# Moving the seventh of seven Strassen products between the fourth and the fifth, with its weight sum written over another tile

## The chip, the cores and the metric

The kernel runs on one core of a Trainium2 chip. The metric is device time in microseconds (us) of one execution. Engines are named as the profile names them: PE is the matrix engine (PEld its weight loads), DVE the vector engine, ACT the scalar engine, POOL the engine that issues some of the transfers here, and SP issues most of them.

## The reference

The reference is a trunk of two transformer layers over 512 tokens of width 1024, in float32. Each layer has an attention part (not touched here) and a gated feed-forward part with a hidden width of 2816:

```python
def swiglu(h, w_gate, w_up, w_down):
    return (jax.nn.silu(h @ w_gate) * (h @ w_up)) @ w_down

# in each layer
h = rms_norm(x, ffn_pre_g[layer])
f = swiglu(h, ffn_w_gate[layer], ffn_w_up[layer], ffn_w_down[layer])
x = x + rms_norm(f, ffn_post_g[layer])
```

## The kernel before

**Precision.** Each float32 operand of a matrix product is split into a rounded high half and the remainder (`split`, lines 143 to 145): ACT casts the high half (L144), DVE subtracts to get the low one (L145). Each product is then three matmuls: high by high, high by low, low by high. In the profile the weights' halves are `whi` and `wlo`, those of the activations `xh`, `xl`, `th` and `tl`.

**Pairs and their seven products.** The hidden width is cut into 22 blocks of 128. Four are computed directly; the other 18 are taken two at a time, as nine pairs, in `products`, which runs once in each layer. For a pair, gate and up weights together with the tokens' two halves (`A0`, `A1`, 256 columns each) form a 2 by 2 block product, which Winograd's form of Strassen's scheme computes with seven products instead of eight. A product, numbered j from 0 to 6, is 24 matmuls of 128x256 (two blocks `e`, four slices of the depth, three halves each). "Place" below means the position in the order of execution, from first to seventh. Before, product j stands at place j + 1.

**The weight side.** Class `Pair` loads four quarters of 128x1024: up's first quarter (`raw[4]`), up's second (`raw[5]`), gate's first (`raw[1]`) and gate's second (`raw[2]`). Product 0 uses the sum of the two up quarters, held in a tile with the tag `sum` (two buffers). Product 3 uses that sum plus gate's first quarter, product 6 that plus gate's second, both written in place in the same `sum` tile. Product 4 uses up's first quarter plus gate's first, written over up's first. Products 1, 2 and 5 use plain quarters. Each sum is one DVE addition of 128x1024 (L174). Up's first quarter has a tag with two buffers (`sum2`), the other three quarters share five (`raw`). A load, issued by SP (L162), waits until its buffer's last reader is done.

**The feed.** `Feed` holds the plan of all weight tiles in the order of their use. `next(1024, 2)` hands out the split weights for one product and has the split of the product two places later recorded; the split halves have three buffers each, so a split at place n + 2 can only begin when the product at place n - 1 has ended.

**The banks.** Products 1, 3, 4 and 5 add up in one pair of PSUM banks (`al`), products 0 and 6 in another (`be`), product 2 alone in a third (`ga`). What each leaves is taken out at once, one half `e` at a time: product 0 is copied to `u[:, A1]` (ACT), 1 to `t[:, A0]` (ACT), 2 is added to `t[:, A0]` (DVE, "gate add"), 3 is copied to `t[:, A1]` (ACT, L1497), 4 is added to `u[:, A1]` (DVE, "up add", L1499), 5 is copied to `u[:, A0]` (ACT, L1501), and 6 is added to `t[:, A1]` (DVE, L1503). As the banks keep adding up, product 4 must not touch a half of `al` before the copy of product 3 has read it, and product 5 not before the up add of product 4 has. Behind product 6 come a multiplication by `rb` (L1504), the activation (ACT, L1505), the product of gate and up (`hd`, L1507) and, once in a pair, four small differences for the down product (L1202 to L1205). Those last rows and the `hd` products are what `Hidden` collects for `down`.

**The order.** The framework that builds the program lays out each engine's instructions from the recorded ones by its own list scheduling; at run time each engine works strictly in that order. An instruction can so stand ahead of one that was recorded earlier.

Of the kernel before, what the change touches and what calls it, by code (L numbers as in the profile page):

```python
# [10 lines left out]
F32 = mybir.dt.float32  # L11
# [7 lines left out]
D, S, P = 1024, 512, 128  # L19
# [49 lines left out]
def trunk(ctx: ExitStack, tc: tile.TileContext, a, out):  # L69
    nc = tc.nc  # L70
# [11 lines left out]
    def name_(n):  # L82
        uid[0] += 1
        return f"{n}_{uid[0]}"

    def U(dt=F32, name="u"):
        return up.tile([P, S], dt, tag="u", name=name_(name), bufs=NU)
# [4 lines left out]
    def bank(tag="mm", name="b"):  # L92
        return ps.tile([P, S], F32, tag=tag, name=name_(name), bufs={"mm": 4, "s": 2, "t": 2}[tag])
# [57 lines left out]
    class Pair:  # L151

        def __init__(self, src):
            self.src, self.raw = src, {}

# [13 lines left out]
        def sums(self, j):  # L172
            def plus(t, x, y):
                V.tensor_tensor(t, x, y, op=OP.add)  # L174

            r = self.raw
            if j == 0:
                r[0] = r[3] = r[6] = wide[0].tile([P, 1024], F32, tag="sum", name=name_("raw"), bufs=2)
                plus(r[0], r[4], r[5])
            elif j in (3, 6):  # L180
                plus(r[j], r[j], r[j // 3])
            elif j == 4:
                plus(r[4], r[4], r[1])

    wide = [None]

    class Down:
# [41 lines left out]
        def plus(self, j, i, x, y):  # L229

            x, t = self.at[x, i], self.at[y, i]
            n = max(len(x), len(t))
            cut_ = lambda v: v if len(v) == n else [v[0][:, c * S:c * S + S] for c in range(n)]
            for p, q in zip(cut_(t), cut_(x)):
                V.tensor_tensor(p, p, q, op=OP.add)
            self.at[j, i] = t
# [15 lines left out]
    class Feed:  # L252
# [8 lines left out]

        def add_pair(self, src):

            for j in range(7):
                self.plan.append((Pair(src) if not j else self.plan[-1][0], 1024, j, None))

        def add_down(self, src):
# [128 lines left out]
    def cut(t, c):  # L396
        return t[0][:, c], t[1][:, c]
# [97 lines left out]
    class Head:  # L495
# [3 lines left out]
        def __init__(self, qk, bt, scale, pv, sums):  # L499
            self.qk, self.bt, self.scale, self.pv, self.sums = qk, bt, scale, pv, sums  # L500
            self.p, self.pt = {}, None
# [538 lines left out]
    def start_a(h):  # L1040
# [12 lines left out]
        def pv(pth, ptl):  # L1053
            fill.until("v")
            o = bank()
            v_ = slice(h * VD, (h + 1) * VD)
            for kt in range(NQT):
                q_ = slice(kt * P, S)
                mm3(o[:, q_], (va[kt][:, 0, v_], va[kt][:, 1, v_]), (pth[:, kt, q_], ptl[:, kt, q_]),
                    kt == 0, kt == NQT - 1)  # L1060
            V.reciprocal(sums, sums)
            of = U(name="of")
            nc.scalar.copy(of, o)

            def rest():
                V.tensor_tensor(of, of, spread(sums), op=OP.mult)
                oh, ol = U(F32R, "oh"), U(F32R, "ol")
                split(oh, ol, of)
                osp.append((oh, ol))

            return rest
# [11 lines left out]
    def ffn(i, x_src, osp, firsts, late=()):  # L1083
# [55 lines left out]
        for f in range(N_WHOLE):  # L1139
# [13 lines left out]
            if f == 1:  # L1153
                next(more)
        products(xs, tb, rb, hid)
        post = (AfterLast if i else After)(i, eps, H)
        down(hid, post)
# [86 lines left out]
    A0, A1 = HALF  # L1244
# [214 lines left out]
    def products(xs, tb, rb, hid):  # L1459

        K2 = KT // 2
        moving = [[cut(tb[k][0], A0) for k in range(K2)], [cut(xs[k], A0) for k in range(K2)],
                  [cut(xs[k + K2], A0) for k in range(K2)], [cut(tb[k][0], A1) for k in range(K2)],
                  [cut(tb[k][1], A0) for k in range(K2)], [cut(tb[k][1], A1) for k in range(K2)],
                  [cut(xs[k + K2], A1) for k in range(K2)]]
        pairs = (NF - N_WHOLE) // 2
        for p in range(pairs):
            al, ga = [], []
            be = [bank("t" if p % 2 else "s", "be") for _ in range(2)]
            gate = [U(name="gt") for _ in range(2)]  # L1470
            up_ = [U(name="ut") for _ in range(2)]
            for j in range(7):
                w = feed.next(1024, 2)
                if p + 1 == pairs and j >= 4:
                    hid.ahead(j // 5)
                if j == 1:
                    al = [bank(name="al") for _ in range(2)]
                if j == 2:
                    ga = [bank(name="ga") for _ in range(2)]
                to = (be, al, ga, al, al, al, be)[j]  # L1480
                for e in range(2):
                    o = to[e][:, A0]
                    for k in range(K2):
                        l, r = w(e * S + k * P, P), moving[j][k]
                        first_ = j < 3 and k == 0
                        for n, (c, d) in enumerate(((0, 0), (0, 1), (1, 0))):
                            nc.tensor.matmul(o, l[c], r[d], start=first_ and n == 0, stop=k == K2 - 1 and n == 2,  # L1487
                                             skip_group_check=True)
                    t, u = gate[e], up_[e]
                    if j == 0:  # L1490
                        nc.scalar.copy(u[:, A1], o)
                    elif j == 1:
                        nc.scalar.copy(t[:, A0], o)
                    elif j == 2:
                        V.tensor_tensor(t[:, A0], t[:, A0], o, op=OP.add)
                    elif j == 3:
                        nc.scalar.copy(t[:, A1], o)  # L1497
                    elif j == 4:
                        V.tensor_tensor(u[:, A1], o, u[:, A1], op=OP.add)  # L1499
                    elif j == 5:  # L1500
                        nc.scalar.copy(u[:, A0], o)  # L1501
                    else:
                        V.tensor_tensor(t[:, A1], t[:, A1], o, op=OP.add)  # L1503
                        V.tensor_tensor(t, t, rb, op=OP.mult)  # L1504
                        nc.scalar.activation(t, t, AF.Silu)  # L1505
                        h = hid.room()
                        V.tensor_tensor(h, t, u, op=OP.mult)  # L1507
                        hid.add(h)
# [275 lines left out]
```

## Time and profile before

| What | Value |
| --- | --- |
| Runs shown (three) | 1115.43, 1115.44 and 1116.55 us, median 1115.44 |
| The profiled execution: span from first to last instruction | 1112.9 us |
| Outside the span, by the median | 2.5 us |
| Gate and up products, layer 0 | 236 to 415.6 us of the span |
| Gate and up products, layer 1 | 816 to 996 us |
| Weight loads of the pairs (`raw<-in_w_pair`) | 72, of 512 KB each |
| DVE sums of weights (L174) | 72, median 1.216 us |
| Up adds (L1499) | 36, of 128x256 |

The profiler records one execution. Times of one row are from its start to its end; on an engine that takes its next instruction before the last one has quite ended, the distance from start to start is the shorter one, and it is the one to add up. A wait in brackets names how long the engine was idle before the row and what ended it. The lines themselves stand in the prediction, each where it is used.

### The profile page before, as it was taken

The page shows a single profiled execution, that of the slowest core. Times are in us where ns is not written, and L with a number is a line of the kernel's source. Part 1 is how long each engine was busy: PE and PEld are TensorE (multiplying, and loading weights), DVE is VectorE, ACT ScalarE, POOL GpSimd, SP SyncE. Part 2 cuts the span into 40 slices and gives each one's busy share as a digit, 9 for nine tenths or more (in the row PEclk, how much of TensorE's full clock was granted, in tenths as well). Part 3 has the DMA queues.
Part 4 walks back from the last instruction along what each step waited for, and adds up shares of the span by engine and source line. Part 5 has one row for each costly group of instructions (what it writes and reads, how often), then busy time and mean ns, then how long its engine had stood idle before and what let it go on. Part 6 is the DMA issues. An engine that isn't in the chain of part 4 may idle for free.

```text
span 1112.9 us, 18983 instructions
## 1 busy us (share of the span) xinstructions
PE 1100.7 (99%) x6973; PEld 983.8 (88%) x6973; DVE 931.1 (84%) x1671; ACT 685.6 (62%) x1339; POOL 68.5 (6%) x106
## 2 busy tenths in 40 slices
PE   9999999999999999999999999999999999999997
PEld 6888889999999998888888888889999999998885
DVE  7788737999989889978868878658999899889977
ACT  6576637755555556768636777666755555566675
POOL 1200000000000002400000000000000000002402
PEclk9999999999999999999999999999999999999999
DMA  7433226423332358970556665635422322459923
GB/s 237 117 107 81 72 72 213 133 73 108 95 125 96 126 168 240 148 213 28 186 152 170 156 181 146 152 121 176 141 76 95 133 81 97 137 170 294 172 55 77
DMA packets 62990, 150.85 MB, mean 136 GB/s; under 512 B 8432, under 2 KB 10224, under 8 KB 62896
## 3 DMA queue, kind: packets, MB, share of 16 engines
q1 hardware_dynamic: 55552, 136.61, 39.0%
q0 software_dynamic: 6912, 12.59, 6.9%
q8 instruction: 55, 0.90, 0.3%
q10 hardware_dynamic: 432, 0.44, 0.1%
q14 instruction: 39, 0.32, 0.1%
HBM read 119.52 MB, written 9.63 MB: 116 GB/s over the span
## 4 chain that ended last, share of the span: by engine, by line
PE 91%; DVE 3%; DMA 2%; issue 1%; ACT 1%; POOL 0%; SPq 0%; POOLq 0%; DVEq 0%; ACTq 0%
PE al L1487 17%; PE b L361 11%; PE b L362 11%; PE b L363 11%; PE be L1487 9%; PE al L1237 8%; PE be L1237 5%; PE ga L1487 4%; PE de L1237 3%; PE ga L1237 3%; PE pt L523 2%; DMA x<-in_x 1%; DVE wlo L145 1%; PE b L1643 1%; PE b L1642 1%
## 5 line engine op out<-in xcount | busy, mean ns | idle before, releaser
L144 ACT CAST whi<-raw 128x1024 fp32r<-128x1024 f32 (+3 forms) x224 | 225.2, 1007 | 203.8 <-PE al L1487 72.2
L145 DVE TENSOR_TENSOR wlo<-raw,whi 128x1024 fp32r<-128x1024 f32 (+3 forms) x224 | 260.6, 1165 | 52.2 <-ACT whi L144 51.3
L1487 PE MATMUL al<-th,whi 128*128 128x256 f32 x432 | 122.8, 284 | 0.2 <-DVE ut L1499 0.2
L1487 PE MATMUL al<-tl,whi 128*128 128x256 f32 x432 | 120.8, 280 | 0.0
L1487 PE MATMUL al<-th,wlo 128*128 128x256 f32 x432 | 120.8, 280 | 0.0
L361 PE MATMUL b<-xh,whi 128*128 128x512 f32 (+1 forms) x298 | 114.5, 385 | 0.0
L363 PE MATMUL b<-xh,wlo 128*128 128x512 f32 (+1 forms) x298 | 110.0, 369 | 0.3 <-DVE wlo L145 0.3
L362 PE MATMUL b<-xl,whi 128*128 128x512 f32 (+1 forms) x298 | 109.9, 369 | 0.0
L174 DVE TENSOR_TENSOR raw<-raw,raw 128x1024 f32<-128x1024 f32 x72 | 86.4, 1217 | 0.6 <-DMA raw<-in_w_pair 0.4
L1487 PEld LDWEIGHTS al<-th,whi 128*128 128x128 f32 x432 | 81.2, 188 | 2.5 <-DVE ut L1499 0.5
L1487 PEld LDWEIGHTS al<-tl,whi 128*128 128x128 f32 x432 | 81.3, 188 | 0.0
L1487 PEld LDWEIGHTS al<-th,wlo 128*128 128x128 f32 x432 | 81.2, 188 | 0.1
L511 ACT ACTIVATE p<-p,mn 128x128 f32<-128x128 f32 (+1 forms) x96 | 54.0, 562 | 39.5 <-DVE mn L509 38.6
L145 DVE TENSOR_TENSOR ptl<-pt,pth 128x128 fp32r<-128x128 f32 (+1 forms) x96 | 46.6, 486 | 29.4 <-ACT pth L144 23.6
L145 DVE TENSOR_TENSOR wlo<-wd,whi 128x512 fp32r<-128x512 f32 x86 | 56.4, 684 | 14.4 <-ACT whi L144 14.2
L144 ACT CAST whi<-wd 128x512 fp32r<-128x512 f32 x86 | 50.0, 619 | 25.5 <-PE al L1237 10.6
L363 PEld LDWEIGHTS b<-xh,wlo 128*128 128x128 f32 x298 | 56.2, 189 | 10.0 <-DVE wlo L145 0.7
L361 PEld LDWEIGHTS b<-xh,whi 128*128 128x128 f32 x298 | 56.4, 189 | 6.4 <-ACT whi L144 0.4
L362 PEld LDWEIGHTS b<-xl,whi 128*128 128x128 f32 x298 | 56.5, 189 | 5.6
L144 ACT CAST pth<-pt 128x128 fp32r<-128x128 f32 (+1 forms) x96 | 40.2, 420 | 26.9 <-PE pt L523 26.1
L1237 PE MATMUL al<-whi,ph 128*128 128x512 f32 x132 | 51.7, 392 | 0.0
L1237 PE MATMUL al<-whi,pl 128*128 128x512 f32 x132 | 51.6, 391 | 0.0
(315 smaller groups left out, 3272.0 us busy)
## 6 DMA issues: line engine op xcount, KB each, us to landing
raw<-in_w_pair SPq DMA_DIRECT2D x72, 512.0 KB, 3.7
wd<-in_w_down SPq DMA_DIRECT2D x54, 256.0 KB, 5.9
raw<-in_w_o SPq DMA_DIRECT2D x16, 512.0 KB, 3.5
raw<-in_w_gu SPq DMA_DIRECT2D x16, 512.0 KB, 3.7
raw<-in_w_down SPq DMA_DIRECT2D x16, 512.0 KB, 4.4
raw<-in_w_qkb SPq DMA_DIRECT2D x16, 512.0 KB, 3.7
wd<-in_w_down POOLq DMA_DIRECT2D x22, 256.0 KB, 5.5
wd<-raw POOLq DMA_DIRECT2D x22, 256.0 KB, 4.4
```

What stands on the lines that cost most here:

```text
L144: return (nc.scalar.copy(dst_hi, src), V.tensor_tensor(dst_lo, src, dst_hi.bitcast(F32), op=OP.subtract))
L145: V.tensor_tensor(dst_lo, src, dst_hi.bitcast(F32), op=OP.subtract))
L174: V.tensor_tensor(t, x, y, op=OP.add)
L361: nc.tensor.matmul(o, l[0], r[0], start=start, stop=False)
L362: nc.tensor.matmul(o, l[0], r[1], start=False, stop=False)
L363: last_mm[0] = nc.tensor.matmul(o, l[1], r[0], start=False, stop=stop)
L511: nc.scalar.activation(p[:, :n], p[:, :n], AF.Exp, bias=mn[:, :1], scale=-1.0, accum_out=self.sums[:, qt:qt + 1])
L523: nc.tensor.transpose(t[:, kt * P:(kt + 1) * P], p[:, kt * P:(kt + 1) * P], ident)
L1237: nc.tensor.matmul(to[e], l[c], r[d], start=j < 4 and k == 0 and n == 0, stop=k == NF // 2 - 1 and n == 2, skip_group_check=True)
L1487: nc.tensor.matmul(o, l[c], r[d], start=first_ and n == 0, stop=k == K2 - 1 and n == 2, skip_group_check=True)
L1642: nc.tensor.matmul(o[:, q_], vv, pth[:, kt, q_], start=kt == 0, stop=False)
L1643: nc.tensor.matmul(o[:, q_], vv, ptl[:, kt, q_], start=False, stop=kt == NQT - 1)
```

## The change

The seven products are taken in the order 0, 1, 2, 3, 6, 4, 5. The sum for product 6 is no longer written over the `sum` tile but over gate's second quarter (`raw[2]`), which product 2 has used by then. In `products` the work behind product 6 is divided: the addition, the multiplication by `rb` and the activation stay with it, at the fifth place; the product of gate and up and what follows goes behind product 5, now the last. What a pair's last three places do for the down product (`hid.ahead`) stays at the same places.

```diff
+        ORDER = (0, 1, 2, 3, 6, 4, 5)
...
             if j == 0:
-                r[0] = r[3] = r[6] = wide[0].tile([P, 1024], F32, tag="sum", name=name_("raw"), bufs=2)
+                r[0] = r[3] = wide[0].tile([P, 1024], F32, tag="sum", name=name_("raw"), bufs=2)
                 plus(r[0], r[4], r[5])
-            elif j in (3, 6):
-                plus(r[j], r[j], r[j // 3])
+            elif j == 3:
+                plus(r[3], r[3], r[1])
+            elif j == 6:
+                r[6] = r[2]
+                plus(r[6], r[6], r[3])
...
-            for j in range(7):
+            for j in Pair.ORDER:
                 self.plan.append((Pair(src) if not j else self.plan[-1][0], 1024, j, None))
...
-            for j in range(7):
+            for n_, j in enumerate(Pair.ORDER):
                 w = feed.next(1024, 2)
-                if p + 1 == pairs and j >= 4:
-                    hid.ahead(j // 5)
+                if p + 1 == pairs and n_ >= 4:
+                    hid.ahead(n_ // 5)
...
                     elif j == 4:
                         V.tensor_tensor(u[:, A1], o, u[:, A1], op=OP.add)
-                    elif j == 5:
-                        nc.scalar.copy(u[:, A0], o)
-                    else:
+                    elif j == 6:
                         V.tensor_tensor(t[:, A1], t[:, A1], o, op=OP.add)
                         V.tensor_tensor(t, t, rb, op=OP.mult)
                         nc.scalar.activation(t, t, AF.Silu)
+                    else:
+                        nc.scalar.copy(u[:, A0], o)
                         h = hid.room()
                         V.tensor_tensor(h, t, u, op=OP.mult)
                         hid.add(h)
```

Lines below the first edits move down by two to five: the sums are L176 after the change, the up add L1504, the add of product 6 L1506, the multiplication by `rb` L1507, the last copy L1510, `hd` L1512.

The change also moves what the scheduling puts ahead. Three places matter. The first is DVE in layer 0's fourth pair (gate tiles `gt_3599` and `gt_3600`, up tiles `ut_3601` and `ut_3602`), around the up adds. Before:

```order
L145 TENSOR_TENSOR wlo_3739<-raw_3519,whi_3738 128x1024
L1499 TENSOR_TENSOR ut_3601<-al_3642,ut_3601 128x256
L174 TENSOR_TENSOR raw_4013<-raw_3878,raw_3880 128x1024
L1499 TENSOR_TENSOR ut_3602<-al_3643,ut_3602 128x256
L145 TENSOR_TENSOR wlo_3771<-raw_3768,whi_3770 128x1024
```

And after the change, from the split for the sixth place (`wlo_3709`) to the up adds:

```order
L145 TENSOR_TENSOR wlo_3709<-raw_3384,whi_3708 128x1024
L145 TENSOR_TENSOR wlo_3739<-raw_3386,whi_3738 128x1024
L1506 TENSOR_TENSOR gt_3599<-gt_3599,be_3597 128x256
L1507 TENSOR_TENSOR gt_3599<-gt_3599,bc_2706 128x512
L1506 TENSOR_TENSOR gt_3600<-gt_3600,be_3598 128x256
L176 TENSOR_TENSOR raw_4017<-raw_3878,raw_3880 128x1024
L1507 TENSOR_TENSOR gt_3600<-gt_3600,bc_2706 128x512
L145 TENSOR_TENSOR wlo_3775<-raw_3772,whi_3774 128x1024
L1504 TENSOR_TENSOR ut_3601<-al_3642,ut_3601 128x256
L1504 TENSOR_TENSOR ut_3602<-al_3643,ut_3602 128x256
```

The up adds, which stood directly behind the split for the last place, now stand behind the four rows of product 6, a weight sum (of `raw_3878` and `raw_3880`, the up quarters of the pair after the next) and one more split, that of the next pair's first product (`wlo_3775`). The second and sixth pair of the layer read the same, and so does layer 1.

The second place is DVE in the fifth pair (`gt_3844`), after the change; the third, seventh and eighth pair of each layer read the same in these rows up to the second up add:

```order
L145 TENSOR_TENSOR wlo_3984<-raw_3635,whi_3983 128x1024
L1506 TENSOR_TENSOR gt_3844<-gt_3844,be_3842 128x256
L1507 TENSOR_TENSOR gt_3844<-gt_3844,bc_2706 128x512
L1506 TENSOR_TENSOR gt_3845<-gt_3845,be_3843 128x256
L1507 TENSOR_TENSOR gt_3845<-gt_3845,bc_2706 128x512
L145 TENSOR_TENSOR wlo_4020<-raw_4017,whi_4019 128x1024
L1504 TENSOR_TENSOR ut_3846<-al_3887,ut_3846 128x256
L1504 TENSOR_TENSOR ut_3847<-al_3888,ut_3847 128x256
L176 TENSOR_TENSOR raw_4017<-raw_4017,raw_3915 128x1024
```

Here no weight sum stands among them; the one for the pair after the next has moved behind the up adds.

The third place is PE, between the sixth and the seventh place of the fourth pair. Before, the last matmul of product 5 on `al` is followed by product 6 on `be`, with nothing in between. After the change the sixth place ends with the first row here (product 4, second half):

```order
L1492 MATMUL al_3643<-th_2610,wlo_3709 128x256
L1492 MATMUL be_3842<-th_2596,whi_3774 128x256
L1492 MATMUL be_3842<-tl_2597,whi_3774 128x256
L1492 MATMUL be_3843<-th_2596,whi_3774 128x256
L1492 MATMUL be_3843<-tl_2597,whi_3774 128x256
L1492 MATMUL be_3842<-th_2596,wlo_3775 128x256
L1492 MATMUL be_3842<-th_2600,whi_3774 128x256
L1492 MATMUL be_3842<-tl_2601,whi_3774 128x256
L1492 MATMUL be_3842<-th_2600,wlo_3775 128x256
L1492 MATMUL al_3642<-th_2598,whi_3738 128x256
```

Eight matmuls of the next pair's product 0 (`be_3842`, `be_3843`) now stand ahead of product 5 (the last row). The first four need only the high half of its weights, the fifth also the low one, `wlo_3775`. In the fifth pair and those like it two matmuls, both on the high half, stand there instead of eight; in the first pair of layer 0 it is five, of layer 1 six, and in the last pair two matmuls of the down product, 512 columns wide.

## The prediction

> **What bounds the kernel now.** The page's first two parts say which engine to look at, its fourth whose work makes up the path.
>
> ```profile
> span 1112.9 us, 18983 instructions
> PE 1100.7 (99%) x6973; PEld 983.8 (88%) x6973; DVE 931.1 (84%) x1671; ACT 685.6 (62%) x1339; POOL 68.5 (6%) x106
> PEclk9999999999999999999999999999999999999999
> PE 91%; DVE 3%; DMA 2%; issue 1%; ACT 1%; POOL 0%; SPq 0%; POOLq 0%; DVEq 0%; ACTq 0%
> ```
>
> PE (TensorE) is the path, at a granted clock that stays in the top tenth. Another engine matters only where PE waits for it. The change lies in the gate and up products of both layers, so the next view is the one of windows, over those two stretches.
>
> ```profile
> 236.00:415.60 179.60, 179.60 (x1514) 178.53 (x1513) 164.35 (x227) 99.98 (x158) 0.00 (x0) 1.00 0.36 118
> 816.00:996.00 180.00, 179.75 (x1513) 178.46 (x1513) 164.37 (x227) 99.98 (x158) 0.00 (x0) 1.00 0.36 119
> ```
>
> The columns after the length are PE, PEld, DVE, ACT, POOL, clock, DMA share. DVE is busy 164 of 180 us, so it has under 2 us to spare in each of the nine pairs: a row that comes late there pushes others. The chain in order of time gives one pair's rhythm, and the first and last of the runs that matter.
>
> ```profile
> 264.57 8.72 PE al L1487 x72
> ...
> 333.17 5.63 PE be L1487 x48
> 338.80 2.81 PE al L1487 x24
> 341.62 2.82 PE ga L1487 x24
> 344.44 8.64 PE al L1487 x72
> ...
> 984.48 8.64 PE al L1487 x72
> ```
>
> A product takes 2.82 us, 0.1175 for each of 24 matmuls; seven take 19.74. The run of 72 (places four to six) should take 8.46 and takes 8.64: one stop. There are sixteen such runs, in all pairs but the first of each layer. The timelines of PE and ACT show the stop.
>
> ```profile
> 347.09 0.28 PE L1487 MATMUL al<-th,whi 128*128 128x256 f32 x1
> ...
> 348.38 0.28 PE L1487 MATMUL al<-th,wlo 128*128 128x256 f32 x1
> 348.59 0.39 PE L1487 MATMUL al<-th,whi 128*128 128x256 f32 x1
> 348.81 0.28 PE L1487 MATMUL al<-tl,whi 128*128 128x256 f32 x1
> 347.21 1.05 ACT L144 CAST whi<-raw 128x1024 fp32r<-128x1024 f32 x1 [0.96 <-PE al L1487]
> 348.17 0.36 ACT L1497 COPY gt<-al 128x256 f32<-128x256 f32 x1
> ```
>
> The product in fifth place starts at 347.09, and its second half is due at 348.50. It adds to a bank that ACT must first copy out (L1497); the copy stands behind a cast and ends at 348.53. The matmul starts 0.09 late, and the next follows after 0.22 instead of 0.12: **0.195 us** in all.
>
> **What the change removes.** In fifth place now stands product 6, which goes to `be`; the copy gets a whole product (2.82 us) more. Sixteen stops go: 16 x 0.195 = 3.1 us. Nothing new is late at that place: `be` was copied four products earlier. One larger stop, in layer 1, hangs on the old order too:
>
> ```profile
> 864.94 5.15 DMA raw<-in_w_pair
> 870.22 1.23 DVE L174 TENSOR_TENSOR raw<-raw,raw 128x1024 f32<-128x1024 f32 x1 [0.44 <-DMA raw<-in_w_pair]
> 871.36 0.42 DVE L1499 TENSOR_TENSOR ut<-al,ut 128x256 f32<-128x256 f32 x1
> 871.31 0.28 PE L1487 MATMUL al<-th,wlo 128*128 128x256 f32 x1
> 871.83 0.38 PE L1487 MATMUL al<-th,whi 128*128 128x256 f32 x1 [0.25 <-DVE ut L1499]
> ```
>
> A weight sum stood between the two up adds and waited for its reload; the add ended at 871.78, PE began 0.05 later, 0.4 late, and 0.1 more on restarting: 0.5 us, which I count as gone. It is also a model of what comes: PE stops when the up add is late. Together **-3.6**.
>
> **What it adds: the up add gets late.** Products 4 and 5 still follow each other on `al`, so product 5 still waits for the up adds (L1504 now). But DVE gets more to do ahead of them. The old order had a split, then the add. The new one has the split for the seventh place, two gate adds with their multiplications, the split for the next pair's first product, and then the up add. The trace holds this very row order once, at the end of layer 0's eighth pair.
>
> ```profile
> 348.30 1.22 DVE L145 TENSOR_TENSOR wlo<-raw,whi 128x1024 fp32r<-128x1024 f32 x1 [1.55 <-ACT whi L144]
> 393.89 1.23 DVE L145 TENSOR_TENSOR wlo<-raw,whi 128x1024 fp32r<-128x1024 f32 x1 [0.33 <-ACT whi L144]
> 395.03 0.41 DVE L1503 TENSOR_TENSOR gt<-gt,be 128x256 f32<-128x256 f32 x1
> 395.48 0.69 DVE L1504 TENSOR_TENSOR gt<-gt,bc 128x512 f32<-128x512 f32 x1
> 396.09 0.41 DVE L1503 TENSOR_TENSOR gt<-gt,be 128x256 f32<-128x256 f32 x1
> 396.54 0.69 DVE L1504 TENSOR_TENSOR gt<-gt,bc 128x512 f32<-128x512 f32 x1
> 397.14 1.22 DVE L145 TENSOR_TENSOR wlo<-raw,whi 128x1024 fp32r<-128x1024 f32 x1
> 398.28 0.69 DVE L1507 TENSOR_TENSOR hd<-gt,ut 128x512 f32<-128x512 f32 x1
> ```
>
> Count from the start of the fifth place. The first split can't start before a cast, and the cast not before an earlier product has let go of its buffer: 348.30 - 347.09 = 1.21. From it to the row behind the second split take 398.28 - 393.89 = 4.39. So the first up add starts at 5.60, ends 0.42 later, and PE may start at 6.07. The seventh place is due at 2 x 2.82 = 5.64. The build has seen this and pulls matmuls of the next pair's first product ahead: two in some pairs, which cover PE until 5.64 + 0.235 = 5.87. PE stops for 0.20 and loses 0.11 on restarting: **0.3 us**. These are the short pairs, four in each layer (third, fifth, seventh, eighth): 8 x 0.3 = 2.4 us. The bounds are 0 and, with no cover, 0.54. The lower one is reached when the chain is 0.2 shorter, and two of its rows could make it so:
>
> ```profile
> 335.91 0.74 DVE L1503 TENSOR_TENSOR gt<-gt,be 128x256 f32<-128x256 f32 x2
> 336.57 1.29 DVE L1504 TENSOR_TENSOR gt<-gt,bc 128x512 f32<-128x512 f32 x2
> ```
>
> Two adds that don't wait for each other start 0.33 apart, while the multiplication that waits for the add ahead of it starts 0.45 after it. Without the two waits the chain would be 0.24 shorter. I go by the row that has them. The Trainium skill (VectorE: DVE Perf Modes, "The DRAIN you can't avoid") says that a semaphore behind each vector operation costs nothing extra. By that rule the short pairs would cost nothing and the sum would be 2.4 lower; the trace, 0.45 against 0.33, doesn't agree with it here.
>
> In the first pair five or six matmuls are pulled ahead (0.6 us of cover), in the ninth two of the down product, which are twice as wide (0.45): both cover the add, and I count them at nothing, or 0.5 each without the cover.
>
> **The long pairs** are the second, fourth and sixth of each layer. There the weight sum of the pair after the next (L176, `raw_4017` in the rows on the change) stands between the second gate add and its multiplication, and eight matmuls are pulled ahead, of which the fifth needs the low half that the second split writes. The sum reads up's first quarter, whose load reuses the buffer that the sixth place's split reads; the load goes out when that split ends.
>
> ```profile
> 343.73 1.22 DVE L145 TENSOR_TENSOR wlo<-raw,whi 128x1024 fp32r<-128x1024 f32 x1
> 344.97 0.33 SPq L162 DMA_DIRECT2D raw<-in_w_pair  x1
> DMA to landing us min/median/max: 4.4/4.4/4.4
> ...
> DMA to landing us min/median/max: 3.2/3.9/4.9
> ```
>
> The last two are the landing of that one load and of all 25 pair loads from 256 to 376 us. Behind the short pair's up add (5.60) DVE has no gap: eight rows of 1024 columns at 1.14, two of 512 at 0.60 and eight of 256 at 0.33 stand before this split, 13.0 us, so it starts at 18.6. The next fifth place starts at 19.74 + 0.3 = 20.04: the split runs from -1.4 to -0.2, and the load leaves then. It lands at -0.2 + 4.4 = 4.2. The sum follows 0.13 behind a landing (870.22 against 864.94 + 5.15), at 4.33; without the wait it would start at 1.21 + 1.14 + 0.45 + 0.61 + 0.33 = 3.74. Then 1.14 for the sum, 0.60 for the multiplication: the second split starts at 6.07, ends at 7.29, PE goes on at 7.34. Four matmuls cover it until 5.64 + 0.47 = 6.11. It loses 1.23 + 0.11 = **1.34 us**; the up add is then in time. Six pairs: 8.0 us.
>
> The ends: a landing of 3.5 or less hides the load, and 3.74 leads to 6.75, 0.64 + 0.11 = 0.75 in each pair, 4.5 us. A landing of 5.2 gives 0.8 more in each, 12.8 us. I take 4.4, the row of this very load in the old order.
>
> **The rest costs nothing.** The last vector and scalar work of a pair gets shorter (a copy, a product and four differences behind the last matmul, where two adds, two multiplications and two activations stood ahead), but PE doesn't wait there. The other loads keep their order on SP's queue; a buffer comes free at most one place (2.8 us) later than before, and its data are asked for most of a pair later, or in the down product two products later. If that cover were gone, one late load would cost what the one in layer 1 cost, 0.5 us.
>
> **Sum:** 8.0 + 2.4 - 3.6 = +6.8 us on the span of 1112.9. The runs' median, 1115.44, lies 2.5 above the span; with the same 2.5 the forecast is **1122.2 us** (+0.6%).
>
> **Rivals.**
> 1. *The reload is hidden.* It lands in under 3.5 us (3.2 is the least in the rows), and the long pairs fall to 0.75: 4.5 + 2.4 - 3.6 = +3.3, 1118.7. Against it: the load leaves about 1.2 us behind another, and such second loads took 4.4 and 5.15. Chance 0.13.
> 2. *Not slower: the vector chain is shorter than walked.* One mechanism, at the split that opens the chain: when its cast starts. From 0.2 earlier the short stops are gone; from 0.6 earlier, with the sum at 3.1 at the latest, the long ones go too, and -3.6 is left: 1111.8. For it speaks that DVE's own rows leave a gap ahead of that split; against it that the cast's start is tied to PE's release in all pairs of the trace. Between the two, with the chain 0.24 shorter and an early landing, the short pairs cost nothing and the long ones 0.63 (one of the two waits lies ahead of the sum): 3.8 - 3.6 = +0.2, 1115.6, no change. The free semaphore of the Trainium skill (VectorE: DVE Perf Modes, same section) would be such a shortening. Chances: 0.07 for faster, 0.11 for no change.
> 3. *The change doesn't remove what it should.* If another wait of 0.195 stops PE at the fifth place, 3.1 comes back: 1125.3. Nothing in the rows speaks for it. Chance 0.05.
> 4. *The reload is slow,* 5.2 as in layer 1: 12.8 + 2.4 - 3.6 = +11.6, 1127.0. Chance 0.10.
>
> **The numbers.** The forecast itself has 0.54, and a measurement can tell about 0.2% (2.2 us) from no change. Rivals 1, 3 and 4 and the forecast are all slower by more than that: 0.82 together, of which I give 0.02 to no change, as rival 1 ends near that bound. Faster has 0.07, no change 0.13. A range from 1116.5 to 1127.5 leaves out the faster case and most of the no-change one.
>
> **What will show it.** The runs of 72 on `al` are gone, and no copy of the third product's sum is waited for. PE's waits name the up add (L1504) or a split (L145) at the start of the seventh place, about 0.3 us in four pairs and 1.2 to 1.5 in three of each layer; DVE's L176 waits for a pair load in the long pairs. I am wrong if the load lands before the sum asks for it, if DVE's rows up to the up add take less than 4.39 us, or if the stops move to the down products.

## The result, and the profile after

| | kernel before | after the change |
| --- | --- | --- |
| Runs on one chip, median (lowest to highest) | 1115.80 us (1115.43 to 1116.55), 4 runs | 1125.97 us (1123.18 to 1126.39), 4 runs |
| Ratio to before, 95% interval | | 1.0084 (1.0072 to 1.0096) |
| Span of the profiled execution | 1112.9 us | 1124.6 us |
| Products of layer 0, first to last matmul | 179.42 us | 185.21 us |
| Products of layer 1 | 179.83 us | 186.84 us |

The change makes the kernel 0.84% slower. The forecast was 1122.2 us in a range from 1116.5 to 1127.5.

First the head of the page after the change, then the view of windows over the two stretches of products (columns as in the prediction).

```profile
span 1124.6 us, 19006 instructions
PE 1103.1 (98%) x6973; PEld 985.9 (88%) x6973; DVE 934.3 (83%) x1671; ACT 687.0 (61%) x1339; POOL 68.2 (6%) x106
```

```profile
235.94:421.15 185.21, 180.59 (x1515) 178.93 (x1514) 167.93 (x230) 101.42 (x158) 0.00 (x0) 1.00 0.36 116
821.24:1008.09 186.85, 181.96 (x1515) 180.33 (x1513) 168.00 (x230) 101.31 (x158) 0.00 (x0) 0.99 0.37 117
```

PE, which was busy for all of these stretches but 0.25 us, now stands still for 4.6 us in one and 4.9 us in the other. Its waits, and those of DVE, say for whom (engine, line, what it waited for: us in total, times, longest).

```profile
PE be L1492 <- DVE wlo L145: 9.3, 6, 2.2
PE be L1242 <- ACT ph L144: 0.4, 1, 0.4
```

```profile
DVE raw L176 <- DMA raw<-in_w_pair: 6.3, 7, 1.7
```

Six waits for a split's low half, three in each layer, hold most of the loss (9.3 us), and DVE waited for pair loads seven times. DVE's timeline in layer 0's fourth pair shows how one of them comes about (start, duration, engine, line, operation, in brackets the idle time before it and what ended it).

```profile
310.92 1.23 DVE L145 TENSOR_TENSOR wlo<-raw,whi 128x1024 fp32r<-128x1024 f32 x1 [1.25 <-ACT whi L144]
312.06 0.42 DVE L1506 TENSOR_TENSOR gt<-gt,be 128x256 f32<-128x256 f32 x1
312.51 0.69 DVE L1507 TENSOR_TENSOR gt<-gt,bc 128x512 f32<-128x512 f32 x1
313.12 0.41 DVE L1506 TENSOR_TENSOR gt<-gt,be 128x256 f32<-128x256 f32 x1
314.25 1.23 DVE L176 TENSOR_TENSOR raw<-raw,raw 128x1024 f32<-128x1024 f32 x1 [0.72 <-DMA raw<-in_w_pair]
315.39 0.69 DVE L1507 TENSOR_TENSOR gt<-gt,bc 128x512 f32<-128x512 f32 x1
316.00 1.22 DVE L145 TENSOR_TENSOR wlo<-raw,whi 128x1024 fp32r<-128x1024 f32 x1
317.13 0.75 DVE L1504 TENSOR_TENSOR ut<-al,ut 128x256 f32<-128x256 f32 x2
```

PE at the same place, and in the fifth pair, one of the short ones:

```profile
315.70 0.28 PE L1492 MATMUL be<-tl,whi 128*128 128x256 f32 x1
317.27 0.39 PE L1492 MATMUL be<-th,wlo 128*128 128x256 f32 x1 [1.29 <-DVE wlo L145]
317.49 0.28 PE L1492 MATMUL be<-th,whi 128*128 128x256 f32 x1
...
336.74 0.28 PE L1492 MATMUL be<-tl,whi 128*128 128x256 f32 x1
337.06 0.38 PE L1492 MATMUL al<-th,whi 128*128 128x256 f32 x1
337.28 0.28 PE L1492 MATMUL al<-tl,whi 128*128 128x256 f32 x1
```

The weight sum (314.25) has waited 0.72 for its load. The split behind it ends at 317.22, and PE, which has done four of the pulled matmuls, goes on at 317.27. A stop is read from the steps between starts: 317.27 - 315.70 = 1.57 in place of 0.1175, then 0.22 in place of 0.1175, together 1.56 us lost. In the fifth pair the steps are 0.32 and 0.22: 0.31 lost. The table has the same reckoning for all pairs with a stop at the seventh place.

| us lost | 2nd pair | 4th | 6th | 3rd, 5th, 7th, 8th together | 1st |
| --- | --- | --- | --- | --- | --- |
| layer 0 | 2.42 | 1.56 | 1.35 | 1.12 | 0.15 |
| layer 1 | 2.51 | 1.77 | 1.33 | 1.12 | 0.14 |

### The profile page after: what moved, and what is told of

Its sections match the earlier page's. It is cut to its first block, busy times and chain, and to the rows that moved or that the text cites. A ratio compares the mean times of both kernels' runs of the same rounds, so it can differ in the third digit from the quotient of the medians.

```text
span 1124.6 us, 19006 instructions
## 1 busy us (share of the span) xinstructions
PE 1103.1 (98%) x6973; PEld 985.9 (88%) x6973; DVE 934.3 (83%) x1671; ACT 687.0 (61%) x1339; POOL 68.2 (6%) x106
## 5 line engine op out<-in xcount | busy, mean ns | idle before, releaser
L176 DVE TENSOR_TENSOR raw<-raw,raw 128x1024 f32<-128x1024 f32 x72 | 87.2, 1218 | 6.4 <-DMA raw<-in_w_pair 6.3
```

## The experiments

Nine edited kernels and the changed one again were run, each beside runs of the kernel before on the same chip (1115.3 to 1115.9 us). The theory was that of the prediction: the loss is what stands ahead of the up add on DVE, that is a split in all pairs, and a weight sum with its reload in three. The rival was that the new order, or the buffers it frees later, costs by itself. All are edits of the changed kernel unless a line says otherwise.

| Kernel | Median us | Ratio to before, 95% interval |
| --- | --- | --- |
| weight sum and split moved behind the up add | 1113.94 | 0.9986 (0.9977 to 0.9995) |
| weight sum alone | 1115.39 | 0.9994 (0.9986 to 1.0003) |
| split alone | 1125.61 | 1.0091 (1.0077 to 1.0105) |
| weight sum, second pair only | 1122.81 | 1.0064 (1.0050 to 1.0078) |
| the new order with the old sums | 1123.59 | 1.0072 (1.0059 to 1.0085) |
| the old order with the new sum | 1125.17 | 1.0088 (1.0075 to 1.0101) |
| split behind the first up add, sum behind the split | 1111.53 | 0.9969 (0.9957 to 0.9981) |
| split behind the second up add, sum behind the split | 1110.74 | 0.9961 (0.9948 to 0.9974) |
| the kernel before, copy ahead of the cast | 1123.15 | 1.0071 (1.0057 to 1.0085) |
| the changed kernel again | 1125.61 | 1.0093 (1.0073 to 1.0112) |

### Both rows behind the up add

```diff
             if j == 0:
                 r[0] = r[3] = wide[0].tile([P, 1024], F32, tag="sum", name=name_("raw"), bufs=2)
-                plus(r[0], r[4], r[5])
+                with behind(up_add[0]):
+                    plus(r[0], r[4], r[5])
...
-                w = feed.next(1024, 2)
+                w = feed.next(1024, 1 if j == 4 else 2)
...
-                        V.tensor_tensor(u[:, A1], o, u[:, A1], op=OP.add)
+                        add = V.tensor_tensor(u[:, A1], o, u[:, A1], op=OP.add)
+                        up_add[0] = add
+                        if not e:
+                            feed.behind[feed.pos + 1] = (add,)
+                            feed.ahead(1)
```

> Edit: after the change, with two rows of VectorE moved: the sum of two up quarters (L176) recorded behind the pair's last up add, and the split of the next pair's first product recorded behind the pair's first up add. Theory (the loss is what stands ahead of the up add on VectorE): the up add starts one split (1.14 us) earlier and never behind a reload, so no stop at the seventh place in any pair; the sixteen stops of 0.195 and the one of 0.5 stay removed: 3.6 us less than before, about 1112.2 us. Rival (the order of the products, or what the buffers are then released by, costs by itself, whatever stands ahead of the up add): the stops go to other places, and the time stays above 1120 us.

The stops at the seventh place are gone in all 18 pairs, and those at the fifth stay gone, so what stands ahead of the up add was the cause. The gain is about half of what was expected (ratio 0.9986, so 1.6 us of 1115.9, where 3.6 were expected). Two things take the rest. One is a new small stop: DVE's rows behind the first up add, and PE at the start of the fifth pair.

```profile
312.18 0.42 DVE L1506 TENSOR_TENSOR ut<-al,ut 128x256 f32<-128x256 f32 x1
312.51 1.21 DVE L176 TENSOR_TENSOR raw<-raw,raw 128x1024 f32<-128x1024 f32 x1
313.65 2.35 DVE L145 TENSOR_TENSOR wlo<-raw,whi 128x1024 fp32r<-128x1024 f32 x2
...
314.96 0.35 PE L1494 MATMUL be<-th,wlo 128*128 128x256 f32 x1
315.15 0.28 PE L1494 MATMUL be<-th,whi 128*128 128x256 f32 x1
```

The split for the next pair's first product now stands behind two sums, and the third matmul, the first to need its low half, costs a step of 0.19 (315.15 - 314.96). This is so in eight pairs, 0.07 to 0.11 each, 0.7 in sum. The other is the pace: the matmuls that follow each other without a stop are 118.1 ns apart on average, before 117.6; over 3024 of them that is 1.4 us (last section). 3.6 - 0.7 - 1.4 = 1.5, and in the profile the products of both layers are 1.7 us shorter than before (the whole span 1.3).

### The weight sum alone

The edit is the first hunk above, with `up_add[0]` set at the up add.

> Edit: after the change, with the sum of two up quarters (L176) alone recorded behind the pair's last up add; the split of the next pair's first product still stands ahead of the up adds. Theory: the six long stops (10.9 us in the trace after the change) become short ones. Seven pairs of each layer then have stops of about 0.28 us: 14 x 0.28 = 3.9, less the 3.6 removed: +0.3 on before, about 1116.1 us. No stop is longer than 0.5 us, so the 16 slow matmuls behind the 2.5 us stop are not there either. Rival (the reload is late for some other reader, or the slow clock comes with the order): 1120 to 1126 us.

1115.39 us. The stops of 1.3 to 2.5 us are gone; seven pairs of each layer have steps of 0.25 to 0.32 followed by 0.22 at the seventh place. So the weight sum makes a pair long. The short stops are left, fourteen of 0.24 to 0.31 us, and together they cost about what the change removed.

### The split alone

The edit is the other two hunks of the first experiment, without `up_add`.

> Edit: after the change, with the split of the next pair's first product alone recorded behind the pair's first up add; the weight sum stands where it is put, now in six pairs of each layer ahead of the second multiplication, and the up add directly behind that. Theory: the short stops go, but in twelve pairs the up add waits for the sum, and the sum for its reload: it may start 1.14 earlier than the split behind which it stood, so each stop is about 1.2 less than a long one (1.35 to 2.5 in the trace): 0.3 to 1.3 us, 12 x 0.7 = 8.4, less 3.6: about 1120.6 us (1116 to 1127). Rival (the split, not the reload, is what the long pairs wait for): no stop, about 1112 us.

1125.61 us, near the upper end of what was expected. PE's waits, and DVE in the fourth pair:

```profile
PE al L1492 <- DVE ut L1504: 8.7, 12, 1.4
```

```profile
313.55 1.23 DVE L176 TENSOR_TENSOR raw<-raw,raw 128x1024 f32<-128x1024 f32 x1 [0.52 <-DMA raw<-in_w_pair]
314.69 0.69 DVE L1510 TENSOR_TENSOR gt<-gt,bc 128x512 f32<-128x512 f32 x1
315.30 0.42 DVE L1504 TENSOR_TENSOR ut<-al,ut 128x256 f32<-128x256 f32 x1
```

No split stands ahead of the up add any more, and PE waits for the add itself, twelve times, with steps of 0.63 to 1.71. The rival, that only the split mattered, falls. Freed of the split, the scheduling has put a sum into six pairs of each layer in place of three: the stops are shorter and twice as many.

### The weight sum in the second pair only

```diff
-                plus(r[0], r[4], r[5])
+                with behind(up_add[0] if self.n % 9 == 3 else None):
+                    plus(r[0], r[4], r[5])
```

(`self.n` counts the pairs from zero over both layers. The sum of each layer's fourth pair is recorded there, and it is the one that stood in the second.)

> Edit: after the change, with the sum of two up quarters (L176) recorded behind the last up add in the second pair of each layer only. Theory: the second pair's long stop (2.4 and 2.5 us) goes; the sums then stand ahead of the second multiplication in the third, fifth and seventh pair, whose reloads leave as the fourth's and sixth's did, 1.35 to 1.8 us each: 6 x 1.5 = 9.0, eight short ones 2.2, less 3.6: +7.6, about 1123.4 us; without a stop above 2 us the 16 slow matmuls (1.5 us) are not there. Rival: the first long stop is long because it is the first (the reload chain settles in the pairs behind it): then the third pair has 2.4 us, and the time is 1125 to 1126 us.

1122.81 us. The long pairs are now the third, fifth and seventh, with steps of 1.47 to 1.83, and no stop is above 2 us. The 2.4 us of the second pair thus belong to that pair and its reload, not to whichever comes first.

### The new order with the old sums

```diff
-                r[0] = r[3] = wide[0].tile([P, 1024], F32, tag="sum", name=name_("raw"), bufs=2)
+                r[0] = r[3] = r[6] = wide[0].tile([P, 1024], F32, tag="sum", name=name_("raw"), bufs=2)
...
-                r[6] = r[2]
-                plus(r[6], r[6], r[3])
+                plus(r[6], r[6], r[2])
```

> Edit: the new order of the products with the old place of the seventh product's sum (written over the sum tile again). Theory (the loss comes with the order, whatever tile the sum is written over): VectorE's rows have the sum of up quarters ahead of the second multiplication in three pairs of each layer again (third, fifth and seventh), and the up adds behind the split in all; 6 long stops of 1.35 to 2.5 us, eight short ones: 1122 to 1127 us, as the change itself. Rival (the loss comes with the sum over gate's second quarter, which keeps that buffer longer): as before, 1116 us or less.

1123.59 us: the order is enough to lose 0.7%. The trace also holds a case that the change itself does not have, the weight sum without a wait for its reload. DVE and PE in layer 0's fifth pair:

```profile
332.91 0.41 DVE L1505 TENSOR_TENSOR gt<-gt,be 128x256 f32<-128x256 f32 x1
333.24 1.22 DVE L176 TENSOR_TENSOR raw<-raw,raw 128x1024 f32<-128x1024 f32 x1
334.38 0.69 DVE L1506 TENSOR_TENSOR gt<-gt,bc 128x512 f32<-128x512 f32 x1
334.98 1.22 DVE L145 TENSOR_TENSOR wlo<-raw,whi 128x1024 fp32r<-128x1024 f32 x1
...
335.49 0.28 PE L1491 MATMUL be<-tl,whi 128*128 128x256 f32 x1
336.25 0.39 PE L1491 MATMUL be<-th,wlo 128*128 128x256 f32 x1 [0.49 <-DVE wlo L145]
336.48 0.28 PE L1491 MATMUL be<-th,whi 128*128 128x256 f32 x1
```

The sum starts 0.33 behind the gate add. The stop is 0.64 + 0.11 = 0.75 us, and the other four pairs of this layer have 0.68 to 0.76. That is the number of the prediction's first rival (0.75 with the reload hidden). What a long pair of the changed kernel costs above 0.75, so 0.6 to 1.8 us, is the wait for the reload. Here ten pairs are long (two of layer 1 with 1.1 and 1.5 us, the other eight with 0.7 to 0.8), in place of six, and the first pair of each layer takes some 1.1 us longer than in the kernel before (21.0 against 20.0 and 19.9).

### The old order with the new sum

The edit gives the kernel before the two `elif` branches of the change, for products 3 and 6 (product 6 so no longer shares the `sum` tile), and nothing else.

> Edit: the old order of the products, with the seventh product's sum written over gate's second quarter. Theory (the loss comes with the order): the up adds stand ahead of the seventh product's rows as before, so nothing stops at the seventh place by them: 1115 to 1118 us. Rival (the place of the sum costs by itself: it keeps a buffer of the raw tiles until the seventh product's split, and VectorE's rows come in another order, two sums between the up adds and the splits): the splits for the sixth and seventh place get up to one sum (1.14 us) late in eight pairs of each layer, 16 x 0.8: about 1128 us.

1125.17 us, between the two expectations and near the rival. I had held the order to be the whole cause; this shows that the other part costs as much by itself. DVE's and PE's waits:

```profile
DVE raw L174 <- DMA raw<-in_w_pair: 25.8, 14, 3.0
```

```profile
PE al L1490 <- DVE ut L1502: 3.3, 9, 0.4
PE al L1490 <- DVE wlo L145: 2.3, 4, 0.9
```

Weight sums wait fourteen times for a load, up to 3.0 us, because here they stand ahead of splits and of product 6's rows; what is queued behind them comes late, up adds and splits in turn. Alone, the parts cost 0.7 and 0.9%, together 0.8%: the costs don't add up, as each edit makes the scheduling place the weight sum anew.

### The sum behind the split

From the first experiment: the weight sum is recorded behind the split of the next pair's first product (`low` holds it) in place of the up add.

```diff
-                with behind(up_add[0]):
+                with behind(low[0]):
                     plus(r[0], r[4], r[5])
...
-                            split(pieces[c // w][0][:, :m], pieces[c // w][1][:, :m], raw[:, c:c + m])
+                            b = split(pieces[c // w][0][:, :m], pieces[c // w][1][:, :m], raw[:, c:c + m])[1]
+                            if isinstance(src, Pair) and not gain:
+                                low[0] = b
```

> Edit: as the kernel with both rows moved, but the sum of two up quarters recorded behind the split of the next pair's first product instead of behind the up add. VectorE's rows are then: first up add, that split, second up add, sums. Theory: in the kernel with both rows moved that split came 0.08 to 0.11 us late behind two sums, and PE stopped that long in the first product of eight pairs; the split now runs 1.1 us earlier, and these 0.75 us go: 1113.2 us, if PE's pace (117.3 or 118.7 ns for a matmul, whole products long) is mixed as there; 1112 if it is the faster one throughout, 1114.5 if the slower. Rival: the pace is slower because PE no longer stops: then fewer stops give nothing, 1114 us or more, with 118.7 in nearly all products.

1111.53 us, faster than both kernels. DVE's rows behind the first up add, and the windows over the products:

```profile
330.70 1.22 DVE L145 TENSOR_TENSOR wlo<-raw,whi 128x1024 fp32r<-128x1024 f32 x1
331.83 0.42 DVE L1508 TENSOR_TENSOR ut<-al,ut 128x256 f32<-128x256 f32 x1
332.17 1.22 DVE L176 TENSOR_TENSOR raw<-raw,raw 128x1024 f32<-128x1024 f32 x1
```

```profile
235.66:413.61 177.95, 177.95 (x1514) 177.74 (x1513) 167.04 (x230) 102.72 (x158) 0.00 (x0) 1.00 0.39 121
813.70:991.53 177.83, 177.83 (x1514) 177.68 (x1513) 167.04 (x230) 102.69 (x158) 0.00 (x0) 1.00 0.40 123
```

All pairs but the first of layer 0 and the last of each layer take 19.71 or 19.72 us from first matmul to first matmul. The products of both layers are 3.5 us shorter than before (359.25 - 355.78), although two matmuls of the down product, 512 columns wide, now stand among them in each layer (0.9 us in all). Like for like they are 4.4 us shorter: 3.6 of removed stops, as the prediction had it, and 0.8 of a quicker pace (steps of 117.4 ns on average, before 117.6). Nearly all products run at the quicker pace, so the rival, that PE is slower when it never stops, falls.

With `if e:` in place of `if not e:` the split goes behind the second up add:

> Edit: as the last one, but the split recorded behind the pair's second up add. VectorE's rows are then: both up adds, the splits for the next pair's first and second product, and the sums behind the next pair's gate adds. Theory: both up adds and both splits are in time, no stop in any pair: 1112 to 1114.5 us as above. Rival: the sum, now ahead of the split for the fifth or sixth place, waits there for its reload, and that split is late by up to 1.1 us: 12 x 1.1 = 13 us more, about 1126 us.

1110.74 us, no stops either, pairs of 19.71 or 19.72 too; the two can't be told apart by their intervals. The rival's wait for a reload didn't come about: DVE doesn't wait for a pair load in this trace.

### The old order without the old stop

From the kernel before:

```diff
                     elif j == 3:
-                        nc.scalar.copy(t[:, A1], o)
+                        feed.behind[feed.pos + 2] = (nc.scalar.copy(t[:, A1], o),)
```

> Edit: the kernel before, old order and old sums, with one thing changed: the cast (and split) of the product two places behind the fifth is recorded behind the copy of the fourth product's second half (L1497), so that the copy stands ahead of the cast on ScalarE. Theory: the stop of 0.195 us at the fifth place comes from that order on ScalarE alone, so the sixteen stops go without any change of the products' order: 3.1 us less, about 1112.2 us. Rival: the cast and split for the seventh place come 0.36 us later and that, or VectorE's rows (a weight sum now stands between the two gate adds in six pairs), stops PE elsewhere: no gain, 1115 us or more.

1123.15 us: the rival. The stops at the fifth place are gone, so the copy behind the cast was their cause. But the cast starts 0.37 us later, the split and the up add with it, and PE stops as long at the sixth place, in all sixteen pairs. DVE and PE in the fifth pair (the last row is product 5's first matmul on `al`):

```profile
328.60 1.23 DVE L145 TENSOR_TENSOR wlo<-raw,whi 128x1024 fp32r<-128x1024 f32 x1 [1.81 <-ACT whi L144]
329.75 0.42 DVE L1499 TENSOR_TENSOR ut<-al,ut 128x256 f32<-128x256 f32 x1
...
330.02 0.28 PE L1487 MATMUL be<-xl,whi 128*128 128x256 f32 x1
330.22 0.39 PE L1487 MATMUL al<-th,whi 128*128 128x256 f32 x1
```

The larger loss is elsewhere: the scheduling also changed the last pair's rows, and from the last product to the end of the down products it takes 6.1 us more in the two layers. The pace of the last section adds 2.0 us in the products (118.3 ns, before 117.6). So this run shows the cause of the old stop, but not what the old order would give without both.

### The changed kernel again

> The changed kernel once more, unedited, for a second profile. If the half clock (3.41 us long in the first profile, at 862.30) follows when a long stop lies within one of the 3.41 us stretches in which the clock is recorded, it is there behind a second pair's stop of 2.4 us or more that lies in one stretch, and not behind one that lies across two; the long stops are again 1.35 to 2.5 us, 10.9 in sum (9.5 to 12). If it has nothing to do with the stops, it is at another place or not there with the same stops. Time: 1125.5 us, with runs of 1123 and 1126 apart by one half clock (1.7 us) each.

1125.61 us; long stops of 2.36, 1.31 and 1.51 us in layer 0, 2.21, 1.46 and 1.36 in layer 1, 10.2 in sum. The half clock is at the same place as in the first profile, behind the stop of 2.21 us that lies in one stretch and not behind the one of 2.36 that lies across two (last section). So the rule of the one stretch held, while a stop of less than the expected 2.4 us was enough. The four runs took 1123.5, 1124.8, 1126.4 and 1129.6 us at mean granted clocks of 0.998, 0.998, 0.997 and 0.996; one half clock more is 1.7 of 1125 us, 0.0015, so part of the spread is that, and the rest is not explained.

## Why the prediction was right, and where its sizes were off

| Term | Forecast, us | Measured in the profile, us |
| --- | --- | --- |
| removed stops | -3.6 | -3.6 (no step above 0.15 at the fifth place) |
| short pairs | +2.4 | +2.2 |
| long pairs | +8.0 | +10.9 (10.2 in the second profile) |
| first pairs | 0 | +0.3 |
| half clock behind a long stop | not foreseen | +1.5 |
| steps without a stop | 0 | +0.5 (117.8 ns on average, before 117.6) |
| the down products | 0 | -0.1 |
| sum | +6.8 (span) | +11.7 (1124.6 - 1112.9) |

The down products are counted here with the two matmuls that stand among the last products of each layer after the change (0.9 us in all). PE waits for `ph` at one place of theirs (0.4 us, above), but they are not longer in sum.

By the runs the change costs 10.2 us (1125.97 - 1115.80), which is nearer to the 11.6 of rival 4, the slow reload, than to the 6.8 of the forecast. The way there is another, as the loads show below.

**What it removes** was right: the copy has a product more, and the sixteen stops and the one of 0.5 don't come back; rival 3 is out.

**The short pairs** were right in mechanism and size (0.24 to 0.32, forecast 0.3). They stay when the weight sum alone is moved, and they go when the split alone is moved: the split ahead of the up add makes them. The rule of the Trainium skill that the prediction weighed, that a semaphore behind each vector operation costs nothing extra (VectorE: DVE Perf Modes, "The DRAIN you can't avoid"), would have made them nothing: eight were measured. Rival 2 is out.

**The long pairs** had the right place and mechanism, the weight sum that waits for its reload ahead of the second multiplication. The step that failed is "the load leaves then" with "I take 4.4, the row of this very load in the old order". It held in the sixth pair (1.33 and 1.35, forecast 1.34), roughly in the fourth (1.56 and 1.77) and not in the second. SP's rows of these loads in layer 0, second and fourth pair, with the landing of each:

```profile
267.56 0.33 SPq L164 DMA_DIRECT2D raw<-in_w_pair  x1
DMA to landing us min/median/max: 5.2/5.2/5.2
...
309.70 0.33 SPq L164 DMA_DIRECT2D raw<-in_w_pair  x1
DMA to landing us min/median/max: 4.5/4.5/4.5
```

DVE's split that opens the chain starts at 268.54 in the second pair and at 310.92 in the fourth. So the second pair's load leaves only 0.98 ahead of it, the fourth's 1.22, and it lands in 5.2 rather than 4.5. The sum then waited 1.64 us in place of 0.72:

```profile
272.80 1.23 DVE L176 TENSOR_TENSOR raw<-raw,raw 128x1024 f32<-128x1024 f32 x1 [1.64 <-DMA raw<-in_w_pair]
```

That is 0.92 us more, and the second pair lost 0.86 more than the fourth. In layer 1 the second pair's load leaves 0.75 ahead and lands in 4.9.

The prediction's load leaves 1.41 ahead of that split and lands in 4.4, which is 2.99 behind the split's start. Measured in the trace, the landing is 4.17 and 4.18 behind it in the second pairs, 3.24 and 3.45 in the fourth, 3.03 and 3.08 in the sixth; this is the term that was mis-sized, and its excess over 2.99 (3.2 us in six pairs) is about the excess of the long pairs (2.9). One price for six pairs was too simple: the prediction counted back from one pair's rhythm, and the second pair's load left later than by it. That the first pair, with its own rhythm, makes it late is likely but not tried. Rival 4 (a landing of 5.2) held in one load of six; the others took 4.3 to 4.9.

**What was not in the sum** is the cost of a stop beyond itself, 1.5 us of half clock, and 0.5 us of slower steps (both in the last section).

## What to carry to other kernels

When work is moved to an earlier place, look at the in-order engine that serves it: what it brings along (here four rows, a split and a weight sum) stands ahead of a row that the next product waits for. A list scheduler may put a row that can wait a whole pair, such as a sum with a load behind it, ahead of one that can't; tying the patient rows behind the urgent ones turned 0.84% slower into 0.3 to 0.4% faster than before with the same order of products. The parts of such a change aren't worth their sum, since each edit makes the scheduler place the rest anew: test them apart and together.

## What the hardware showed that I had not expected

**One of the longest stops was followed by half the clock.** The windows of the changed kernel over the two longest stops and behind them:

```profile
271.80:275.20 3.40, 1.87 (x16) 1.67 (x15) 2.40 (x3) 0.59 (x2) 0.00 (x0) 1.00 0.31 118
275.20:278.60 3.40, 2.78 (x23) 2.78 (x24) 3.40 (x5) 1.41 (x3) 0.00 (x0) 1.00 0.00 0
858.90:862.30 3.40, 1.44 (x12) 1.44 (x13) 3.40 (x6) 1.57 (x2) 0.00 (x0) 1.00 0.04 17
862.30:865.70 3.40, 3.40 (x19) 3.40 (x18) 3.18 (x4) 0.38 (x1) 0.00 (x0) 0.50 0.25 52
```

Behind layer 1's stop the granted clock is 0.50 for 3.4 us, and 16 matmuls take 0.213 us each in place of 0.1175: 1.5 us lost. Counted back in steps of 3.41, the stretch ahead of it had PE idle for 1.96 us; in layer 0 the same stop fell across two stretches, idle 1.5 and 0.6, and the clock stayed whole. Both profiles of this kernel show it at the same place, though in the second one layer 0's stop is the longer (2.36 against 2.21), and no kernel with stops under 2 us shows it in its products. The Trainium skill (TensorE: Matmul & The Clock Gate, "What's actually happening") has windows of 3413 ns, which fits these stretches, and asks for at least one idle window before the clock is halved; here 58% of one was enough, and 1.90 us (56%) in the second profile. The ends of other kernels, where PE runs out of work, add two cases: half the clock followed a stretch with 1.97 us idle (the new order with the old sums), while the full clock followed one with 1.93 (the old order with the new sum). So the limit lies near 1.9 us, but idle time read from the profile does not fix it exactly. That the share within a stretch decides is read from these places, not tried by moving a stop.

**PE has two paces at a full granted clock.** The mean step of a product's 24 matmuls is 117.3 ns in some products and 118.5 to 118.9 in others, for many products on end, with changes mostly at stops. Of 126 products 124 and 125 are at the quicker pace in the two kernels without stops, 96 before, 83 after the change, 53 with both rows behind the up add (one to three more or fewer, by where a product that changes midway is counted). The program alone does not set it: the second profile of the changed kernel has 67 where the first has 83. The slower pace costs 1% while it lasts, and in the profile with both rows behind the up add it took 1.4 us of the gain. What sets it is open, and that a stop starts it is not shown.
